# Gate and up projections by Strassen's algorithm, down projection accumulated in DRAM

## The chip, the cores and the metric

The kernel runs on one core of a Trainium2 chip. The metric is the device time of one execution in microseconds (us); of several runs the median is given. The core has five engines that run side by side, each through its own list of instructions in a fixed order: TensorE (PE; its weight loads are shown apart as PEld), VectorE (DVE), ScalarE (ACT), GpSimd (POOL) and SyncE (SP, which only issues DMAs here). An instruction that waits for another engine holds up all that stands behind it on its own.

## The reference

One layer of a decoder for 512 tokens of 2048 features, all in float32. The part that the change touches is the feed-forward network:

```python
z = rmsnorm(h, norm_ffn_g[l])
ff = (jax.nn.silu(z @ w_ffn_gate[l]) * (z @ w_ffn_up[l])) @ w_ffn_down[l]
h = h + ff.astype(h.dtype)
return rmsnorm(h, norm_final_g)
```

Gate and up are 2048 x 5632 each, down is 5632 x 2048. Ahead of it stand a combined input projection, windowed attention, gated linear attention, a gated merge and an output projection with the residual.

## The kernel before, in words

Everything lies with features on the 128 partitions and the 512 tokens along the row. The weights come in pieces of 128 x 1024 float32 (512 KB), in the order of their use; a piece holds, for gate, up and down alike, four blocks of 128 rows by 256 columns.

**Three matmuls for one.** TensorE multiplies in a format of fewer bits (F32R), so both sides are split into a high and a low part: ScalarE casts (high, L196), VectorE subtracts (low, L197). `mm3` (L229 to L233) then adds three products: high x high, high x low, low x high, each a matmul of 128 x 128 weights with 512 columns.

**Pieces.** `load_piece` (L203) asks for the DMA into `wf` and splits it into `wh` and `wl`, three buffers of each. `next_piece` (L217) hands out piece i and asks for the ones up to i + 2; it also takes up other waiting work of the attention part. `project` (L235) gives two banks of 256 output features.

**Feed-forward.** 5632 hidden features go in 11 blocks of 512. `ffn_up` (L856) makes gate and up of a block, in two halves of 256 features: four pieces of gate into two banks, then four of up; VectorE multiplies with the token's inverse rms (`rb2`), ScalarE gives the sigmoid, VectorE the products, and the result is split into `fh` and `fl`. `ffn_down` (L880) takes 8 pieces; for each of 16 output tiles 12 matmuls fill a bank, which VectorE adds to a running sum `acc` in SBUF (L892). The order is up(0), up(1), down(0), up(2), down(1) and so on; the last down is done in two halves of 256 tokens together with the final norm (L937 on).

**Buffers.** Eight banks of PSUM of 128 x 512 float32 take TensorE's results: four under the tag "mm" (all projections), four under "aux" (attention, norms). Tiles of 128 x 512 lie in 66 slots ("t") and 12 work tiles ("w"). A framework puts in all waits: a tile's buffer is given to the next one when its last reader is done, and a static scheduler fixes each engine's order.

In front of the feed-forward, the output projection (L821) leaves the residual stream in `hT`, sends it to DRAM (`h_d`, L827) and splits the gained z at once into `zh`, `zl` (L831 to L839), while the squares for the second norm are summed up.

## Time and profile before

| | us |
|---|---|
| median of three runs | 2664.93 |
| lowest, highest | 2664.81, 2666.26 |
| span of the profiled execution | 2663.9 |

The profile is one execution. Its span runs from the first to the last instruction of the core; the runs' times hold a little more around it, and 2664.93 less 2663.9 is 1.0 us. A page gives busy times by engine, the chain of work that ended last, and groups of instructions: line, engine, operation, what is written from what, count, then busy time and the mean length of one, and the engine's idle time just before them with what ended it. TensorE's matmuls overlap, so the length of one is not its price; that is the step from one start to the next. A timeline row has start and length in us. A row of the windows has, for a stretch, each engine's busy us and count, then PEclk, the TensorE clock that was granted (1.00 is full), the DMA share and GB/s.

### The profile page before, as it was taken

What the parts mean: (1) busy time and instruction counts of PE and PEld (TensorE: products, weight loads), DVE (VectorE), ACT (ScalarE), POOL (GpSimd) and SP (SyncE); (2) the same over time, 40 slices, a digit from 0 to 9 for tenths busy, and PEclk for the clock granted to TensorE, in tenths of its full rate; (3) what the DMA queues carried; (4) which work ended last, traced back from release to release, by engine and by line L of the source; (5) the groups of instructions that cost most, each with busy time, mean ns of one, the idle gap of its engine ahead of it and who ended that gap; (6) DMA issues with size and microseconds to landing.
All of it is one profiled execution on the core that took longest, in us unless ns stands there. A gap on an engine that the chain in (4) does not pass through costs nothing.

```text
span 2663.9 us, 29245 instructions
## 1 busy us (share of the span) xinstructions
PE 2635.0 (99%) x12038; PEld 2188.5 (82%) x12038; DVE 1185.7 (45%) x1690; ACT 753.0 (28%) x1040; POOL 21.4 (1%) x42
## 2 busy tenths in 40 slices
PE   8899999999999999999999999999999999999998
PEld 7777888888888888888888888888888888888887
DVE  6695463733333335444343434444434343434355
ACT  5465222422222223332222222222222222222233
POOL 0000000000000000000000000000000000000001
PEclk9999999999999999999999999999999999999999
DMA  6622223234433333443343233323323232233231
GB/s 193 130 71 71 80 87 95 72 127 133 127 111 111 108 98 107 142 147 103 99 141 117 95 98 101 95 95 96 102 95 95 96 101 96 95 96 102 95 124 67
DMA packets 92070, 280.73 MB, mean 105 GB/s; under 512 B 10512, under 2 KB 18880, under 8 KB 91936
## 3 DMA queue, kind: packets, MB, share of 16 engines
q1 hardware_dynamic: 91936, 278.87, 33.3%
q8 instruction: 94, 1.54, 0.2%
q14 instruction: 40, 0.33, 0.0%
HBM read 263.11 MB, written 15.72 MB: 105 GB/s over the span
## 4 chain that ended last, share of the span: by engine, by line
PE 96%; DMA 1%; DVE 1%; ACT 1%; issue 0%; POOL 0%; SPq 0%; DVEq 0%; ACTq 0%; POOLq 0%
PE ps_fd L232 6%; PE ps_fd L233 6%; PE ps_fd L231 6%; PE ps_fg L233 6%; PE ps_fg L231 6%; PE ps_fg L232 6%; PE ps_fu L233 6%; PE ps_fu L232 6%; PE ps_fu L231 6%; PE ps_ga L231 2%; PE ps_wo L233 2%; PE ps_gb L231 2%; PE ps_ga L232 2%; PE ps_wo L232 2%; PE ps_ga L233 2%; PE ps_gb L233 2%
## 5 line engine op out<-in xcount | busy, mean ns | idle before, releaser
L197 DVE TENSOR_TENSOR wl<-wf,wh 128x1024 fp32r<-128x1024 f32 (+1 forms) x464 | 559.0, 1205 | 1011.0 <-ACT wh L196 1002.6
L196 ACT CAST wh<-wf 128x1024 fp32r<-128x1024 f32 (+1 forms) x464 | 481.3, 1038 | 1535.6 <-PE ps_fd L232 315.5
L231 PE MATMUL ps_fu<-zh,wh 128*128 128x512 f32 x704 | 274.0, 389 | 0.0
L232 PE MATMUL ps_fu<-zl,wh 128*128 128x512 f32 x704 | 274.0, 389 | 0.0
L233 PE MATMUL ps_fu<-zh,wl 128*128 128x512 f32 x704 | 273.9, 389 | 0.0
L231 PE MATMUL ps_fg<-zh,wh 128*128 128x512 f32 x704 | 273.9, 389 | 0.0
L232 PE MATMUL ps_fg<-zl,wh 128*128 128x512 f32 x704 | 273.9, 389 | 0.0
L233 PE MATMUL ps_fg<-zh,wl 128*128 128x512 f32 x704 | 273.9, 389 | 0.0
L231 PE MATMUL ps_fd<-fh,wh 128*128 128x512 f32 x640 | 249.0, 389 | 0.0
L232 PE MATMUL ps_fd<-fl,wh 128*128 128x512 f32 x640 | 249.0, 389 | 0.0
L233 PE MATMUL ps_fd<-fh,wl 128*128 128x512 f32 x640 | 249.0, 389 | 0.0
L892 DVE TENSOR_TENSOR acc<-ps_fd,acc 128x512 f32<-128x512 f32 x160 | 110.5, 691 | 193.7 <-PE ps_fd L233 193.7
L232 PEld LDWEIGHTS ps_fg<-zl,wh 128*128 128x128 f32 x704 | 132.2, 188 | 27.4
L233 PEld LDWEIGHTS ps_fu<-zh,wl 128*128 128x128 f32 x704 | 132.2, 188 | 27.4
L233 PEld LDWEIGHTS ps_fg<-zh,wl 128*128 128x128 f32 x704 | 132.2, 188 | 27.4
L232 PEld LDWEIGHTS ps_fu<-zl,wh 128*128 128x128 f32 x704 | 132.2, 188 | 27.4
L231 PEld LDWEIGHTS ps_fg<-zh,wh 128*128 128x128 f32 x704 | 132.2, 188 | 27.4
L231 PEld LDWEIGHTS ps_fu<-zh,wh 128*128 128x128 f32 x704 | 132.2, 188 | 27.4
L231 PEld LDWEIGHTS ps_fd<-fh,wh 128*128 128x128 f32 x640 | 120.2, 188 | 25.0
L233 PEld LDWEIGHTS ps_fd<-fh,wl 128*128 128x128 f32 x640 | 120.2, 188 | 24.9
L232 PEld LDWEIGHTS ps_fd<-fl,wh 128*128 128x128 f32 x640 | 120.2, 188 | 24.9
L231 PE MATMUL ps_ga<-uh,wh 128*128 128x512 f32 x256 | 100.1, 391 | 0.0
(264 smaller groups left out, 3992.8 us busy)
## 6 DMA issues: line engine op xcount, KB each, us to landing
wf<-in_pieces_dram SPq DMA_DIRECT2D x448, 512.0 KB, 3.7
x<-in_xT_dram SPq DMA_DIRECT2D x16, 256.0 KB, 4.8
wf<-in_pieces_dram SPq DMA_DIRECT2D x16, 256.0 KB, 4.6
mA_d<-sga SPq DMA_DIRECT2D x16, 256.0 KB, 3.2
ya<-mA_d SPq DMA_DIRECT2D x16, 256.0 KB, 3.0
hT<-in_xT_dram SPq DMA_DIRECT2D x16, 256.0 KB, 3.6
h_d<-hT SPq DMA_DIRECT2D x16, 256.0 KB, 3.3
acc<-h_d SPq DMA_DIRECT2D x16, 256.0 KB, 4.8
```

The source lines that it names most:

```text
L196: nc.scalar.copy(dst_hi, src)
L197: nc.vector.tensor_tensor(out=dst_lo, in0=src, in1=dst_hi.bitcast(F32), op=ALU.subtract)
L231: nc.tensor.matmul(ps, lhsT=ah, rhs=bh, start=first, stop=False)
L232: nc.tensor.matmul(ps, lhsT=ah, rhs=bl, start=False, stop=False)
L233: nc.tensor.matmul(ps, lhsT=al, rhs=bh, start=False, stop=last)
L892: nc.vector.tensor_tensor(out=acc[m], in0=bank, in1=acc[m], op=ALU.add)
```

## The change

**Gate and up together by Strassen's algorithm (Winograd's form).** The left side is z: 512 tokens in two halves, times pairs of feature tiles (`za`, `zb`). The right side is a pair of weight blocks of gate and of up. Seven products replace eight; each has 256 tokens. A row of the tile `zs` holds the high part of such a left side in its first 256 columns and the low part in the others. One matmul of 512 columns multiplies both with the high weights, a second one of 256 columns adds low weights x high side onto the first half of the bank; the two halves of a bank are added when it is read ("fold").

**Weights.** A piece now holds, for four row blocks, 128 columns of gate and of up (quads). `load_quads` splits the first three quarters as they are, forms four sums in place, and splits all of it again: two tiles `wh` and two `wl` a piece, of four buffers each (three before); `wf` has two buffers (three before).

**One pair.** `ffn_pair` makes 128 hidden features from four pieces with seven banks: four aux (products 0, 2, 4, 6), three mm (1, 3, 5). VectorE then combines the banks, folds them and applies norm, sigmoid and product. A block has four pairs.

**Left sides.** `strassen_side` builds the seven sides for a pair of feature tiles; three of the eight pairs of tiles as the output projection goes on, five behind it. z is scaled by the first norm's `rb1`, and the second norm is divided by it again.

**Down.** Its bank is copied by ScalarE into a work tile, and GpSimd issues a DMA that adds it onto `h_d` in DRAM. The running sums are read back ahead of the last block. The order is four pairs of block 0, then for each block: the first pair of the next block, down, three more pairs. There are 11 work tiles instead of 12.

```diff
-N_LONG, N_SHORT = 66, 12
+N_LONG, N_SHORT = 66, 11
+KEPT = 6
...
+    def load_quads(i, wf, wh, wl):
+        nc.sync.dma_start(wf, pieces[i])
+        split(wh[:, 0 : 6 * P], wl[:, 0 : 6 * P], wf[:, 0 : 6 * P])
+        b11, b21, b22, b12 = (wf[:, n * 2 * P : (n + 1) * 2 * P] for n in range(4))
+        tt = nc.vector.tensor_tensor
+        tt(out=b11, in0=b11, in1=b12, op=ALU.add)
+        tt(out=b12, in0=b12, in1=b22, op=ALU.add)
+        tt(out=b22, in0=b11, in1=b22, op=ALU.add)
+        tt(out=b21, in0=b22, in1=b21, op=ALU.add)
+        th = wpool.tile([P, CW], F32R, tag="wh", name=f"th_{i}")
+        tl = wpool.tile([P, CW], F32R, tag="wl", name=f"tl_{i}")
+        split(th, tl, wf)
...
+    def strassen_side(j, za, zb):
+        s12, s34 = work(f"s12_{j}"), work(f"s34_{j}")
+        tt = nc.vector.tensor_tensor
+        tt(out=s12[:, one], in0=zb[:, two], in1=za[:, two], op=ALU.subtract)
...
+        for i, side_ in enumerate(sides):
+            t = slot(f"zs_{j}_{i}", F32R)
+            split(t[:, one], t[:, two], side_)
+            zs[j].append(t)
...
+        if m0 < KEPT:
+            strassen_side(m0 // 2, *pair)
+        else:
+            late.append((m0 // 2, *pair))
+    for pair in late:
+        strassen_side(*pair)
...
+    def ffn_pair(blk, j):
+        outs = [(mm_bank if i % 2 else aux_bank)(f"ps_fu{blk}_{j}_{i}") for i in range(7)]
+        for k0 in range(0, KD // 2, 2):
+            raw, sums = next_quads()
+            for i, (hl, at) in enumerate(
+                ((raw, 0), (raw, 1), (raw, 2), (sums, 0), (sums, 3), (sums, 2), (sums, 1))
+            ):
+                bank = outs[i]
+                for kp in range(2):
+                    k = k0 + kp
+                    z = zs[k][i]
+                    wh, wl = (t[:, at, kp] for t in hl)
+                    if k < KD // 2 - 1:
+                        nc.tensor.matmul(bank, lhsT=wh, rhs=z, start=k == 0, stop=False)
+                        nc.tensor.matmul(bank[:, one], lhsT=wl, rhs=z[:, one], start=False, stop=False)
+                    else:
+                        nc.tensor.matmul(bank[:, one], lhsT=wl, rhs=z[:, one], start=False, stop=False)
+                        nc.tensor.matmul(bank, lhsT=wh, rhs=z, start=False, stop=True)
...
+        nc.scalar.copy(u, outs[0])
+        tt(out=c, in0=outs[1], in1=u, op=ALU.add)
+        fold(g[:, one], c)
+        tt(out=u, in0=u, in1=outs[5], op=ALU.subtract)
+        tt(out=u3, in0=outs[4], in1=u, op=ALU.add)
+        tt(out=c2, in0=outs[6], in1=u3, op=ALU.add)
+        fold(g[:, two], c2)
+        tt(out=u3, in0=outs[3], in1=u3, op=ALU.add)
+        fold(up[:, two], u3)
+        tt(out=u, in0=outs[3], in1=u, op=ALU.add)
+        tt(out=u, in0=outs[2], in1=u, op=ALU.add)
+        fold(up[:, one], u)
+        tt(out=g, in0=g, in1=rb2, op=ALU.mult)
...
-                    mm3(bank, wh[:, j, ws], wl[:, j, ws], fh[j], fl[j], j == 0, j == 3)
-                if blk == 0:
-                    acc[m] = slot(f"acc_{m}")
-                    nc.sync.dma_start(acc[m], h_d[m])
-                nc.vector.tensor_tensor(out=acc[m], in0=bank, in1=acc[m], op=ALU.add)
+                    mm3(bank, wh[:, j, ws], wl[:, j, ws], *f[j], j == 0, j == 3)
+                part = work(f"fd_{blk}_{m}")
+                nc.scalar.copy(part, bank)
+                nc.gpsimd.dma_start(h_d[m], part, accum_op=ALU.add)
...
+    ff = [ffn_pair(0, j) for j in range(4)]
+    for blk in range(NB - 1):
+        nxt = [ffn_pair(blk + 1, 0)]
+        ffn_down(blk, ff)
+        nxt += [ffn_pair(blk + 1, j) for j in range(1, 4)]
+        ff = nxt
```

In the changed file, L208 and L209 are the split, L238 to L241 the four sums, L944 to L948 the product matmuls, L956 the fold of two halves, L958 ScalarE's copy of product 0, L959 to L976 the rest of the combination (L968 is the last reader of product 2, L972 allots the sigmoid's tile), L993 the copy of a down bank and L994 the accumulating DMA.

## The prediction

> **What bounds the kernel now.** I read the page first (busy shares, then the chain), then the groups by form, then TensorE's, VectorE's and the clock's rows in time.

> ```profile
> span 2663.9 us, 29245 instructions
> PE 2635.0 (99%) x12038; PEld 2188.5 (82%) x12038; DVE 1185.7 (45%) x1690; ACT 753.0 (28%) x1040; POOL 21.4 (1%) x42
> PE 96%; DMA 1%; DVE 1%; ACT 1%; issue 0%; POOL 0%; SPq 0%; DVEq 0%; ACTq 0%; POOLq 0%
> L231 PE MATMUL ps_fu<-zh,wh 128*128 128x512 f32 x704 | 274.0, 389 | 0.0
> ```

> TensorE is the bound, and its column "idle before" is 0.0: in gate and up (six groups of 704) it never waits. The 389 ns are the length of one overlapped matmul; the price is the step from start to start, so TensorE's timeline, the first and last of 31 matmuls of 512 columns and of 19 of 256 (with nothing else between):

> ```profile
> 1219.83 0.39 PE L233 MATMUL ps_fg<-zh,wl 128*128 128x512 f32 x1
> ...
> 1226.63 0.39 PE L233 MATMUL ps_fg<-zh,wl 128*128 128x512 f32 x1
> ...
> 2634.72 0.28 PE L231 MATMUL ps_fd<-fh,whd 128*128 128x256 f32 x1
> ...
> 2636.88 0.28 PE L231 MATMUL ps_fd<-fh,whd 128*128 128x256 f32 x1
> ```

> 6.80/30 = 0.2267 us and 2.16/18 = 0.120 us: the short one costs little over half, its own weight load included.

> **TensorE's work.** Before: 11 blocks x 8 feature tiles x 16 x 3 = 4224 steps, 957.6 us. Now: 44 pairs (one call of ffn_pair each) x 4 pieces x 7 products x 2, that is 2464 long and 2464 short steps, 2464 x 0.3467 = 854.3 us. Gain 103.3. A pair is 56 x 0.3467 = 19.4 us, a piece 4.85. [...]

> **VectorE's work.** Groups by form, then VectorE's timeline (first column start, second length):

> ```profile
> L197 DVE TENSOR_TENSOR wl<-wf,wh 128x1024 fp32r<-128x1024 f32 x448 | 548.2, 1224 | 1009.6 <-ACT wh L196 1001.2 <-PE ps_att L663 8.4
> L892 DVE TENSOR_TENSOR acc<-ps_fd,acc 128x512 f32<-128x512 f32 x160 | 110.5, 691 | 193.7 <-PE ps_fd L233 193.7
> L953 DVE TENSOR_TENSOR osum<-osum,osq 128x256 f32<-128x256 f32 x28 | 12.4, 442 | 10.7 <-ACT osq L951 10.7
> L196 ACT CAST wh<-wf 128x1024 fp32r<-128x1024 f32 x448 | 471.7, 1053 | 1531.6 <-PE ps_fd L232 315.5 <-PE ps_fg L232 299.3 <-PE ps_fu L232 203.2
> L735 ACT COPY ob<-ps_ob 128x512 f32<-128x512 f32 x8 | 4.7, 586 | 4.0 <-PE ps_ob L727 4.0
> ```
> ```profile
> 1512.81 0.69 DVE L873 TENSOR_TENSOR u<-ps_fu,rb 128x512 f32<-128x512 f32 x1
> 1513.54 0.69 DVE L874 TENSOR_TENSOR u<-u,g 128x512 f32<-128x512 f32 x1
> 1514.14 1.22 DVE L197 TENSOR_TENSOR wl<-wf,wh 128x1024 fp32r<-128x1024 f32 x1
> 1515.28 0.68 DVE L197 TENSOR_TENSOR fl<-u,fh 128x512 fp32r<-128x512 f32 x1
> ```

> Independent instructions overlap by 0.09: steps 0.60 (512) and 1.14 (1024); one that reads the result just ahead of it starts 0.73 behind. The same 0.09 off the lengths gives 0.36 for 256 columns and 0.87 for 768 (0.955 long, between the lengths for 512 and 1024). A piece now costs VectorE 0.87 + 4 x 0.36 + 1.14 = 3.45, where it cost 1.14; a pair's fold (L956 to L976 and one split) is 4 x 0.36 + 12 x 0.60 = 8.6. A pair asks 4 x 3.45 + 8.6 = 22.4 us of VectorE at the very least, against TensorE's 19.4. VectorE, 45% busy overall, becomes the slower engine in this stage; the projection down, where it has room, can prepare only two pieces ahead (four hi buffers, two a piece).

> **Where the wait lies.** Seven of eight banks are in use, and even-numbered products share four, so product 2 of a pair needs the bank whose last reader is L968 of the pair before. Before, on TensorE, gate to up, and now, pair 5_3 to pair 6_0 (block and pair):

> ```order
> L232 MATMUL ps_fg5_1_1_12760<-zl_15_8661,wh_323_12792 128x512
> L233 MATMUL ps_fg5_1_1_12760<-zh_15_8660,wl_323_12793 128x512
> L231 MATMUL ps_fu5_1_0_12891<-zh_0_7643,wh_324_12822 128x512 [waits Activation_49]
> L232 MATMUL ps_fu5_1_0_12891<-zl_0_7644,wh_324_12822 128x512
> L233 MATMUL ps_fu5_1_0_12891<-zh_0_7643,wl_324_12823 128x512 [waits DVE_49]
> ```
> ```order
> L948 MATMUL ps_fu5_3_6_15088<-zs_7_6_8864,th_335_15141 128x512
> L945 MATMUL ps_fu6_0_0_15285<-zs_0_0_7661,wl_336_15175 128x256 [waits DVE_49]
> L944 MATMUL ps_fu6_0_0_15285<-zs_1_0_7828,wh_336_15174 128x512
> L945 MATMUL ps_fu6_0_0_15285<-zs_1_0_7828,wl_336_15175 128x256
> L945 MATMUL ps_fu6_0_1_15286<-zs_0_1_7664,wl_336_15175 128x256
> L944 MATMUL ps_fu6_0_1_15286<-zs_1_1_7831,wh_336_15174 128x512
> L945 MATMUL ps_fu6_0_1_15286<-zs_1_1_7831,wl_336_15175 128x256
> L944 MATMUL ps_fu6_0_2_15287<-zs_0_2_7667,wh_336_15174 128x512 [waits DVE_49,PE_49]
> ```

> After a pair's end TensorE has 0.9 us of work, then stands at product 2 (the last row) with everything queued behind it. VectorE, the fold of pair 5_2 between loads of pieces (c, u, uu, u3, cc, g are the fold's tiles, wl and tl lows of raw and summed weights):

> ```order
> L959 TENSOR_TENSOR c_5_2_15058<-ps_fu5_2_1_14880,uu_5_2_15054 128x512 [waits DMASW5_49,PE_49,Activation_49]
> L956 TENSOR_TENSOR g_5_2_15056<-c_5_2_15058 128x256 [waits DMASW6_49,DMASW3_49,DVE_49]
> L209 TENSOR_TENSOR tl_331_14939<-wf_331_14928,th_331_14938 128x1024 [waits Activation_49]
> L209 TENSOR_TENSOR wl_332_14972<-wf_332_14970,wh_332_14971 128x768 [waits DMAHW7_49,Activation_49]
> L238 TENSOR_TENSOR wf_332_14970<-wf_332_14970 128x256 [waits DVE_49]
> L239 TENSOR_TENSOR wf_332_14970<-wf_332_14970 128x256 [waits DVE_49]
> L961 TENSOR_TENSOR uu_5_2_15054<-uu_5_2_15054,ps_fu5_2_5_14884 128x512 [waits DMASW4_49,PE_49]
> L240 TENSOR_TENSOR wf_332_14970<-wf_332_14970 128x256 [waits DVE_49]
> L962 TENSOR_TENSOR u3_5_2_15055<-ps_fu5_2_4_14883,uu_5_2_15054 128x512 [waits DMASW7_49,DVE_49]
> L241 TENSOR_TENSOR wf_332_14970<-wf_332_14970 128x256 [waits DVE_49]
> ```
> ```order
> L963 TENSOR_TENSOR cc_5_2_15059<-ps_fu5_2_6_14885,u3_5_2_15055 128x512 [waits DVE_49,PE_49]
> L956 TENSOR_TENSOR g_5_2_15056<-cc_5_2_15059 128x256 [waits DVE_49]
> L965 TENSOR_TENSOR u3_5_2_15055<-ps_fu5_2_3_14882,u3_5_2_15055 128x512
> L209 TENSOR_TENSOR tl_332_14981<-wf_332_14970,th_332_14980 128x1024 [waits Activation_49]
> L209 TENSOR_TENSOR wl_333_15014<-wf_333_15012,wh_333_15013 128x768 [waits DMAHW0_49,Activation_49]
> L956 TENSOR_TENSOR u_5_2_15057<-u3_5_2_15055 128x256 [waits DVE_49]
> L238 TENSOR_TENSOR wf_333_15012<-wf_333_15012 128x256 [waits DVE_49]
> L967 TENSOR_TENSOR uu_5_2_15054<-ps_fu5_2_3_14882,uu_5_2_15054 128x512
> L239 TENSOR_TENSOR wf_333_15012<-wf_333_15012 128x256 [waits DVE_49]
> L968 TENSOR_TENSOR uu_5_2_15054<-ps_fu5_2_2_14881,uu_5_2_15054 128x512 [waits DVE_49]
> ```

> From L959 to the end of L968: 7 x 0.60 + 9 x 0.36 + 2 x 1.14 + 2 x 0.87 = 11.5, with 0.4 for instructions that read their neighbour's result: 11.9 us. L959 in turn starts behind ScalarE's copy of product 0 (L958), and that product closes in the pair's fourth piece. So the pairs form a loop. From L968, TensorE has five products of the first piece (3.5), two pieces (9.7), two steps taken early (0.45) and the rest of product 0 (0.47): 14.1. The matmul's end adds 0.16 (0.39 less 0.227), the copy 0.6 (0.586 by L735). 11.9 + 14.9 = **26.8 us a pair instead of 19.4**, a gap of 7.4. Where the order puts product 3 ahead of product 2 (the second pair of a stage) it is 0.7 less, since one product fewer lies behind L968; I take 7.0 throughout. The first pair behind each projection down has two prepared pieces and does not wait; the down phases leave stages of 5, nine times 4, and 3 pairs, so 44 - 11 = 33 pairs wait: **+231 us**. Bounds: 11.9 could be 10.5 (neighbours' waits free, rows closer) or 13.5 (every instruction at 0.04 over its length), 33 x 1.5 = 50 either way.

> **The clock.** TensorE's timeline and the windows (PEclk is the column behind POOL) at its one long gap:

> ```profile
> 96.33 0.79 PE L231 MATMUL ps_qa<-uh,wh 128*128 128x512 f32 x1 [6.94 <-ACT wh L196]
> 96.92 0.63 PE L232 MATMUL ps_qa<-ul,wh 128*128 128x512 f32 x1
> 97.35 0.63 PE L231 MATMUL ps_qa<-uh,wh 128*128 128x512 f32 x1
> 97.77 0.63 PE L233 MATMUL ps_qa<-uh,wl 128*128 128x512 f32 x1
> ```
> ```profile
> 90.00:91.00 1.00, 0.00 (x0) 0.00 (x0) 0.00 (x0) 0.00 (x0) 0.00 (x0) 1.00 1.08 232
> 92.00:93.00 1.00, 0.00 (x0) 0.00 (x0) 0.00 (x0) 0.00 (x0) 0.00 (x0) 0.50 0.95 366
> 101.00:102.00 1.00, 1.00 (x4) 0.80 (x3) 0.97 (x2) 0.98 (x2) 0.00 (x0) 0.59 0.91 298
> 102.00:103.00 1.00, 1.00 (x9) 0.85 (x7) 0.97 (x6) 0.08 (x1) 0.00 (x0) 1.00 0.92 197
> ```

> The gap began at 89.39 (96.33 less 6.94); by 92 the granted clock is 0.50, and it stays there until about 101.6. For 5.3 us a step costs 0.425 (97.77 less 96.92, halved) instead of 0.227: 2.5 us lost. The loop's gaps are of that length (6 to 7.4), and what follows lies on the loop, so each should lose 0 to 2.5. I take 2.2, since some gaps are shorter: **+73 us**. [...]

> **Start and end.** Five of eight left sides are built behind the last output projection: 5 x 11 x 256 columns, some 20 us at 0.36, and the third piece's raw low stands behind them. TensorE covers two pieces (9.7) of it: about +14 (10 to 18). At the end no next pair hides the fold, and the last block's weights are split only behind it: from the pair's end some 9 us, a clock loss of 2, a point for the crowded first half: +12 (8 to 18).

> **What costs nothing.** ScalarE copies a down bank (0.586) inside the 2.7 us that TensorE takes for one (12 x 0.2267); VectorE loses L892. The 512 KB of a piece land in 3.7 us behind a free buffer, inside the five that VectorE takes for a piece; with two buffers instead of three there is about 1 us to spare, 33 to 44 us if it goes. Elsewhere one work tile less: 0 (-3 to +5).

> ```profile
> wf<-in_pieces_dram SPq DMA_DIRECT2D x448, 512.0 KB, 3.7
> h_d<-hT SPq DMA_DIRECT2D x16, 256.0 KB, 3.3
> ```

> An accumulating DMA isn't in the trace. The nearest row is a plain write of 256 KB, 3.3 us. ScalarE's later copies reuse a tile whose DMA was issued five banks (13.6 us) before, so the cost is 0 up to four times that row; beyond, the down phase slows. I take 0.

> **The sum.** The runs' median, 2664.9, is 1.0 over the span. 2663.9 + 1.0 - 103.3 + 231 + 73 + 14 + 12 = **2892 us**, called 2890.

> **Rivals.** *Faster:* L968 comes before product 2 is wanted, there is no loop, and 2664.9 - 103.3 + 26 = 2588. It decides at a chain of 11.9 us falling under about 4.5. For it, VectorE idles 55% now; against it, the 22.4 us that a pair asks. 5%. *Loop broken, VectorE saturated:* 22.4 a pair, 33 x 3.0 = 99, 2688; against it, the copy L958 that VectorE must await. 7%. *Loop at full clock:* gaps broken up by odd matmuls keep the clock at 1.00: 2819. For it, only that the trace has a single such gap. 18%. *Accumulation late:* at twice the plain row and one at a time, the twelfth lands 79 us behind the phase's start, and the first fold's last tile (L972) is that one's; it is wanted at some 64 (43.5 of down, 20 of a pair). Ten phases 15 us late: 3040. No row speaks for it. 8%. The forecast keeps 62%.

> **The numbers.** The forecast's own range is 2835 to 2960 (50 for the chain, 20 for the clock). Taking in the full-clock rival with its bound gives 2785 to 2960, leaving out 5 + 7 + 8%. Within 0.2% (5 us), about what a measurement here can tell from no change, only a saturated VectorE with a short start would land: 2%. Faster 6%, slower 92%.

> **What would show it.** Right: TensorE's waits headed by the product matmuls (L944) for VectorE's uu, some 33 of 6 to 9 us; PEclk of 8 or so in the gate and up slices; VectorE at some 1850 us busy (1185.7, less 176 loads of 1.224, 220 instructions of 0.69 and L892's 110.5, plus 176 x 3.95 + 44 x 10.1, lengths and not steps); L958 to L958 of neighbouring pairs 27 to 29 us. Wrong: pairs at 20 us with no gaps; gaps with PEclk at 1.00; ScalarE's L993 waiting for the POOL queue.

## The result and the profile after

The changed kernel takes **2768.8 us** (median of four runs, 2767.4 to 2772.0) against 2665.1 for the one before: 1.039 times as long, 95% interval 1.0376 to 1.0406. The forecast was 2890, with 2785 to 2960 as its range: slower, as said, but by 104 us and not by 225. The page of the profiled execution:

```profile
span 2766.2 us, 33264 instructions
PE 2603.9 (94%) x12742; PEld 2143.9 (78%) x12742; DVE 1774.0 (64%) x2984; ACT 994.0 (36%) x1460; POOL 160.4 (6%) x202
PEclk9999999999999999999999999999999999999998
PE 58%; DVE 23%; issue 12%; ACT 4%; DMA 2%; POOL 0%; ACTq 0%; DVEq 0%; SPq 0%; POOLq 0%
```

TensorE was 96% of the chain of work that ended last and is 58% now; VectorE has 23% of it. VectorE's 1774 us busy are near the forecast's 1850. The granted clock is where it was: no slice of gate and up shows the forecast's 8. TensorE's waits (total, times, longest, in us):

```profile
PE ps_fu L944 <- ACT th L208: 97.4, 113, 2.3
PE ps_fu L944 <- DVE u L962: 14.6, 32, 1.2
PE ps_fu L945 <- DVE wl L209: 11.1, 1, 11.1
```

There is no gap of 6 to 9 us behind VectorE's uu. There are over a hundred short ones, most of them before the first product of a piece's *sums* (th), for their cast. The second row is the wait at product 2: it ends with L962, not with L968, the reader of product 2 that the forecast named. A block in the windows: the pair behind a projection down, the second, the third, and the next block's first pair with the down behind it (second column length, then busy us of TensorE, its weight loads, VectorE, ScalarE, GpSimd; PEclk third from the end):

```profile
1798.43:1818.14 19.71, 19.71 (x113) 17.12 (x112) 13.84 (x21) 8.36 (x10) 0.86 (x1) 1.00 0.46 108
1818.14:1839.09 20.95, 18.61 (x102) 15.44 (x100) 18.81 (x35) 7.08 (x9) 0.00 (x0) 1.00 0.22 74
1839.09:1864.53 25.44, 21.70 (x113) 16.76 (x112) 23.17 (x41) 8.75 (x11) 0.00 (x0) 1.00 0.26 83
1864.53:1889.98 25.45, 21.74 (x113) 16.70 (x112) 23.12 (x41) 8.98 (x11) 0.00 (x0) 1.00 0.25 83
1889.98:1935.47 45.49, 45.49 (x206) 37.77 (x206) 24.37 (x34) 19.00 (x27) 13.00 (x15) 1.00 0.87 197
```

The four pairs and a down take 137.0 us; TensorE's own work in them is 4 x 19.4 + 43.5 = 121.1. So a block loses 15.9 us: nothing to speak of behind a down, 3.5 in the second pair (its window is short by some 2 us of matmuls, which the last row has), 6.0 in the third and 6.1 in the next block's first. Of such a 6.0 TensorE is idle for 3.7 (25.44 less 21.70); 2.0 lie in its busy time, 21.70 for matmuls that take 19.71 in the first row, at full clock, and 0.3 is the first row's own excess over 19.4. Where they wait, VectorE is busy for 23.2 of 25.4 us. In down itself TensorE never waits.

**What sets 25.4 us.** TensorE's waits in one such pair (timeline; the bracket has the idle time before the row and what ended it), two of VectorE's rows, and the chain of work through the same pair:

```profile
1563.79 1.19 PE L944 MATMUL ps_fu<-zs,th 128*128 128x512 f32 x4 [0.45 <-ACT th L208]
1568.65 0.47 PE L944 MATMUL ps_fu<-zs,wh 128*128 128x512 f32 x1 [0.41 <-DVE u L962]
1570.03 0.96 PE L944 MATMUL ps_fu<-zs,th 128*128 128x512 f32 x3 [0.44 <-ACT th L208]
1576.92 1.18 PE L944 MATMUL ps_fu<-zs,th 128*128 128x512 f32 x4 [1.18 <-ACT th L208]
1583.60 1.19 PE L944 MATMUL ps_fu<-zs,th 128*128 128x512 f32 x4 [1.17 <-ACT th L208]
```
```profile
1562.82 0.69 DVE L959 TENSOR_TENSOR c<-ps_fu,uu 128x512 f32<-128x512 f32 x1 [0.75 <-ACT uu L958]
...
1574.02 0.68 DVE L968 TENSOR_TENSOR uu<-ps_fu,uu 128x512 f32<-128x512 f32 x1
```
```profile
1581.96 0.44 DVE wf L241
...
1582.50 1.05 ACT th L208
...
1583.60 1.65 PE ps_fu L944 x6
...
1587.38 0.25 PE ps_fu L948
...
1587.65 0.60 ACT uu L958
...
1588.27 0.70 DVE c L959
```

The forecast's chain from L959 to the end of L968 was 11.9 us, and it is (1562.82 to 1574.70). But product 2 of the next pair starts at 1568.65, six us before L968 ends, on L962, the last reader of product 4. L968's bank goes to a later product, and all that waits for it are weight loads, 22 times in the run and 6.6 us together. The loop closes elsewhere. VectorE works without a long pause from L959 (1562.82) to the last weight sum of the next pair's third piece (L241, ends 1582.40): 19.6 us, the fold and the lows and sums of three pieces mixed in one queue. Then ScalarE casts these sums (1.05, with the hand-overs 1.2), TensorE does the rest of the third piece and the fourth's first product, which closes product 0 (4.0), ScalarE copies it (0.6), and the next L959 starts at 1588.27: 25.45 us. (The first expectation below calls this piece the fourth; it is the third.)

### The profile page after: what moved, and what is told of

Read it like the earlier page. It is cut to its first block, busy times and chain, and to the rows that moved or that the text cites. A ratio compares the mean times of both kernels' runs of the same rounds, so it can differ in the third digit from the quotient of the medians.

```text
span 2766.2 us, 33264 instructions
## 1 busy us (share of the span) xinstructions
PE 2603.9 (94%) x12742; PEld 2143.9 (78%) x12742; DVE 1774.0 (64%) x2984; ACT 994.0 (36%) x1460; POOL 160.4 (6%) x202
## 4 chain that ended last, share of the span: by engine, by line
PE 58%; DVE 23%; issue 12%; ACT 4%; DMA 2%; POOL 0%; ACTq 0%; DVEq 0%; SPq 0%; POOLq 0%
PE ps_fu L944 6%; PE ps_fd L270 6%; PE ps_fd L272 6%; PE ps_fd L271 6%; DVE wl L209 3%; DVE tl L209 3%; ACT th L208 3%; PE ps_fu L945 3%; PE ps_ga L270 2%; PE ps_ga L271 2%; PE ps_gb L270 2%; PE ps_ga L272 2%; PE ps_gb L272 2%; PE ps_gb L271 2%; PE ps_wo L271 2%
## 5 line engine op out<-in xcount | busy, mean ns | idle before, releaser
L209 DVE TENSOR_TENSOR wl<-wf,wh 128x1024 fp32r<-128x1024 f32 (+2 forms) x464 | 511.1, 1102 | 611.6 <-ACT wh L208 603.0
L208 ACT CAST wh<-wf 128x1024 fp32r<-128x1024 f32 (+2 forms) x464 | 442.3, 954 | 799.7 <-DMA wf<-in_pieces_dram 162.2
L944 PE MATMUL ps_fu<-zs,th 128*128 128x512 f32 x1232 | 433.7, 408 | 97.4 <-ACT th L208 97.4
L944 PEld LDWEIGHTS ps_fu<-zs,th 128*128 128x128 f32 x1232 | 222.6, 188 | 172.1 <-ACT th L208 133.6
L944 PE MATMUL ps_fu<-zs,wh 128*128 128x512 f32 x924 | 336.2, 402 | 16.9 <-DVE u L962 14.6
L208 ACT CAST th<-wf 128x1024 fp32r<-128x1024 f32 x176 | 184.5, 1048 | 461.1 <-DVE wf L241 297.4
L945 PE MATMUL ps_fu<-zs,tl 128*128 128x256 f32 x1232 | 313.4, 283 | 0.8 <-DVE tl L209 0.8
L209 DVE TENSOR_TENSOR tl<-wf,th 128x1024 fp32r<-128x1024 f32 x176 | 215.1, 1222 | 129.6 <-ACT th L208 117.7
L945 PE MATMUL ps_fu<-zs,wl 128*128 128x256 f32 x924 | 248.5, 282 | 11.1 <-DVE wl L209 11.1
L945 PEld LDWEIGHTS ps_fu<-zs,tl 128*128 128x128 f32 x1232 | 232.3, 189 | 28.5 <-DVE tl L209 13.7
L944 PEld LDWEIGHTS ps_fu<-zs,wh 128*128 128x128 f32 x924 | 171.9, 188 | 69.9 <-issue 23.2
L994 POOL DMA_DIRECT2D h_d<-fd x160 | 138.9, 912 | 1247.8 <-ACT fd L993 1242.0
L945 PEld LDWEIGHTS ps_fu<-zs,wl 128*128 128x128 f32 x924 | 175.0, 189 | 21.7 <-DVE wl L209 11.4
L993 ACT COPY fd<-ps_fd 128x512 f32<-128x512 f32 x160 | 90.8, 582 | 58.0 <-PE ps_fd L272 58.0
## 6 DMA issues: line engine op xcount, KB each, us to landing
wf<-in_pieces_dram SPq DMA_DIRECT2D x448, 512.0 KB, 3.3
h_d<-fd POOLq DMA_DIRECT2D x160, 256.0 KB, 6.0
x<-in_xT_dram SPq DMA_DIRECT2D x16, 256.0 KB, 4.7
wf<-in_pieces_dram SPq DMA_DIRECT2D x16, 256.0 KB, 4.3
mA_d<-sga SPq DMA_DIRECT2D x16, 256.0 KB, 2.8
ya<-mA_d SPq DMA_DIRECT2D x16, 256.0 KB, 2.9
hT<-in_xT_dram SPq DMA_DIRECT2D x16, 256.0 KB, 3.8
h_d<-hT SPq DMA_DIRECT2D x16, 256.0 KB, 3.4
```

The lines of the kernel that those rows point to most:

```text
L208: nc.scalar.copy(dst_hi, src)
L209: nc.vector.tensor_tensor(out=dst_lo, in0=src, in1=dst_hi.bitcast(F32), op=ALU.subtract)
L944: nc.tensor.matmul(bank, lhsT=wh, rhs=z, start=k == 0, stop=False)
L945: nc.tensor.matmul(bank[:, one], lhsT=wl, rhs=z[:, one], start=False, stop=False)
L993: nc.scalar.copy(part, bank)
L994: nc.gpsimd.dma_start(h_d[m], part, accum_op=ALU.add)
```

## Experiments

Two theories stood at first. **Q**: VectorE's whole in-order queue sets a waiting pair; whatever it sheds or gains per pair the pair does too, down to TensorE's 19.4. **B**: the forecast's loop, through the bank that L968 frees. The kernel before ran beside each experiment, at 2664.9 to 2665.3 us; runs without an interval are single ones.

**e1_two_more: more work for VectorE, behind L968.**

```diff
         fold(up[:, one], u)
+        for _ in range(2):
+            tt(out=c, in0=c2, in1=c2, op=ALU.add)
```

> Two more additions of 128x512 on VectorE in every pair, behind the fold that reads product 2 (nothing uses their result). Theory Q (VectorE's queue: the pair's time is VectorE's work from the first addition of the fold to the last weight sum of the next pair's fourth piece, 19.6 us, then the cast of those sums 1.05, TensorE's last piece 4.1 and ScalarE's copy 0.6, 25.4 together): 1.2 us more in each of the 34 pairs that have gaps now, +41 us, 2800 to 2815. Theory B (the prediction's loop through the bank that L968 frees): the additions stand behind L968, so 2769 as now, 2765 to 2775.

Measured 2838.4. B falls: work behind L968 costs. Q's 1.2 us is exact where the clock stays up (26.66 for 25.44), but the whole is 28 us above the 2810 that Q's 41 give. Windows of e1: such a pair and one that is longer with the same work, then two stretches of 3.41 us around the longest gap of the first and two around that of the second; and the rows that end these gaps in TensorE's timeline:

```profile
1442.01:1468.67 26.66, 21.74 (x114) 16.88 (x113) 24.38 (x43) 8.78 (x11) 0.00 (x0) 1.00 0.24 80
1871.43:1899.67 28.24, 23.31 (x114) 18.09 (x113) 24.38 (x43) 8.79 (x11) 0.00 (x0) 0.94 0.24 75
1458.11:1461.53 3.42, 1.67 (x9) 1.26 (x9) 2.73 (x6) 1.14 (x2) 0.00 (x0) 1.00 0.01 4
1461.53:1464.94 3.41, 2.83 (x15) 2.44 (x16) 2.78 (x4) 1.27 (x2) 0.00 (x0) 1.00 0.20 55
1888.18:1891.60 3.42, 1.14 (x9) 0.78 (x7) 2.16 (x6) 1.77 (x3) 0.00 (x0) 1.00 0.00 0
1891.60:1895.01 3.41, 3.41 (x9) 2.73 (x10) 3.28 (x5) 0.63 (x1) 0.00 (x0) 0.50 0.36 107
```
```profile
1462.11 1.19 PE L944 MATMUL ps_fu<-zs,th 128*128 128x512 f32 x4 [2.28 <-ACT th L208]
...
1891.54 2.04 PE L944 MATMUL ps_fu<-zs,th 128*128 128x512 f32 x4 [2.28 <-ACT th L208]
```

Both gaps are 2.28 us long. After the second the granted clock is 0.50 for 3.41 us, 1.6 us lost (28.24 less 26.66); after the first it stays at 1.00 (the last section shows where the two lie). Over the whole run e1's mean granted clock is 0.981 and the changed kernel's 0.993: of 2836.6 and 2766.2 us that is 53.9 and 19.4 us of clock not granted, some 34 more, enough for the 28. The forecast's clock loss exists, then, but the changed kernel's trace has the clock at 1.00 from 1229.6, in its first pair, to 2693.9, behind its last.

**e2_bank_early: product 2 read early.**

```diff
         tt(out=u, in0=u, in1=outs[5], op=ALU.subtract)
+        u2 = work(f"u2_{blk}_{j}")
+        tt(out=u2, in0=outs[2], in1=u, op=ALU.add)
...
-        tt(out=u, in0=outs[3], in1=u, op=ALU.add)
-        tt(out=u, in0=outs[2], in1=u, op=ALU.add)
-        fold(up[:, one], u)
+        tt(out=u2, in0=outs[3], in1=u2, op=ALU.add)
+        fold(up[:, one], u2)
```

> The fold reads product 2 right behind product 5, three positions and some 6 us earlier, into a tile of its own; as many VectorE instructions as now. Theory B (the bank of L968): the loop of 26.8 us falls below 21 and most gaps go, 2600 to 2680. Theory Q (VectorE's queue): nothing that the queue holds is less, 2755 to 2775, the lower end for TensorE's short waits at products 2 and 6 (0.4 us each).

Measured 2776.5: no gain, if anything 8 us lost, and the third pairs of a stage stay at 25.4. B falls a second time.

**e5_no_sums: the sums left out.**

```diff
-        tt(out=b11, in0=b11, in1=b12, op=ALU.add)
-        tt(out=b12, in0=b12, in1=b22, op=ALU.add)
-        tt(out=b22, in0=b11, in1=b22, op=ALU.add)
-        tt(out=b21, in0=b22, in1=b21, op=ALU.add)
```

> The four weight sums of each piece are left out (the last four products then use the plain weights); all else is as in the changed kernel. Theory Q (VectorE's queue): 16 x 0.36 to 0.44 us less in a pair, 25.4 falls to TensorE's 19.4 to 20, and of the 197 us of gaps in the 44 pairs some 160 go: 2590 to 2630. Theory G (the gaps come from something else on the way, the DMA of a piece or ScalarE's cast behind it): 2700 or more.

Measured 2598.7. A third pair of a stage in it:

```profile
1400.12:1419.83 19.71, 19.71 (x113) 17.14 (x112) 17.18 (x25) 8.99 (x11) 0.00 (x0) 1.00 0.32 106
```

With 6 us less for VectorE, TensorE is never idle in it (nor in any other pair but the first two): the landing of the pieces, the casts and the banks would all have kept up. This is what Q asks, but it isn't Q alone: the sums' place between a piece's two casts goes with their work, and e3 below parts the two. With the sums for nothing, this order of the work would be 66 us under the kernel before.

**e4_down_alone: the kernel before with the new down.** The running sums are read back ahead of the last block.

```diff
...
-                nc.vector.tensor_tensor(out=acc[m], in0=bank, in1=acc[m], op=ALU.add)
+                part = work(f"fd_{blk}_{m}")
+                nc.scalar.copy(part, bank)
+                nc.gpsimd.dma_start(h_d[m], part, accum_op=ALU.add)
```

> The kernel before with the new path of down alone: ScalarE copies each bank, GpSimd issues the adding DMA, the running sums are read back once ahead of the last block. Prediction's price of this part, 0: 2660 to 2670. If the adding DMAs or the copies were part of the loss: 2680 or more.

Measured 2672.4, 7 us more. Four of them are two waits early in the last down (first row, 1.2 and 2.5), for the cast of its weights, whose landings are issued between and behind the read-back's 16 transfers; this down's matmuls are busy for 2.4 us more as well (111.3 for 108.9 before). In the changed kernel the adding DMAs land in 6.0 us (second row), nearly twice the plain write's 3.4, and no listed wait is for them.

```profile
L231 PE MATMUL ps_fd<-fh,whd 128*128 128x256 f32 x128 | 37.4, 292 | 4.0 <-ACT whd L196 3.8 <-DVE acc L948 0.2
```
```profile
h_d<-fd POOLq DMA_DIRECT2D x160, 256.0 KB, 6.0
```

**e12_three_landing: three buffers for the landing piece, nine work tiles.**

```diff
-N_LONG, N_SHORT = 66, 11
+N_LONG, N_SHORT = 66, 9
...
-        wf = wpool.tile([P, CW], F32, tag="wf", name=f"wf_{i}", bufs=2)
+        wf = wpool.tile([P, CW], F32, tag="wf", name=f"wf_{i}", bufs=3)
```

> The changed kernel with three landing buffers as before the change instead of two (nine work tiles instead of eleven). Theory Q: VectorE's queue has the same work, so nothing: 2755 to 2775. If the two buffers cost the 33 to 44 us that the prediction put on them in case: 2725 to 2740.

Measured 2762.9. Of the 6 us, 4.6 are gained ahead of the feed-forward (its first matmul starts at 1199.4 instead of 1204.1); the pairs are as long as before. Two landing buffers cost the changed kernel nothing in the pairs, as forecast.

**e3_sums_pool: the sums on GpSimd**, in `load_quads`.

```diff
-        tt = nc.vector.tensor_tensor
+        tt = nc.gpsimd.tensor_tensor
```

> The four sums of a piece (L238 to L241) go on GpSimd instead of VectorE. Theory Q: VectorE loses 16 x 0.36 to 0.44 = 5.8 to 7.0 us a pair, 25.4 falls to TensorE's 19.4 plus small gaps, and some 150 of the 197 us of gaps go: 2600 to 2640, under the kernel before, if GpSimd takes no more than the 0.75 us of its one 128x256 row each (3.2 us a piece against 4.85 on TensorE). Theory B: only the nine sums between L959 and L968 count, 3.2 us a pair, 2650 to 2680. If GpSimd's sums slow down VectorE, or stand behind its DMA issues in the down stages, above 2680.

Measured 2937.0 (1.102, interval 1.1003 to 1.104), 300 us off. Q as stated counted work and forgot the order. The chain through one piece of e3:

```profile
1959.50 1.05 ACT th L208
...
1960.57 0.59 DVE tl L209
...
1961.71 0.68 DVE fl L209
1962.40 0.88 DVE wl L209
...
1963.35 0.74 POOL wf L238
...
1965.78 0.74 POOL wf L241
...
1966.55 1.06 ACT th L208
```

From one cast of sums to the next 7.05 us pass: VectorE's queue holds the next piece's low behind this piece's, the sums wait for that low, the cast for the sums. While VectorE stands for GpSimd it can't go on to another piece. (Part of the 168 us over the changed kernel is the clock: the mean granted clock is 0.969 here and 0.993 there.) Q needs the clause that a piece's steps form a chain through this queue.

**e7_ahead: the split of the sums issued behind the next piece's raw split.**

```diff
...
-        split(th, tl, wf)
+        if pending:
+            split(*pending.pop())
+        pending.append((th, tl, wf))
...
```

> The split of a piece's sums is issued behind the raw split of the next piece, so that VectorE has the next piece's low (0.87 us) to do while ScalarE casts the sums (1.05 us). Theory Q with the waits in VectorE's own order (1.19 us once a pair behind the last sum, 0.75 for ScalarE's copy): 25.4 falls to about 24.2, 34 x 1.2 = 40 us less, 2720 to 2740. If only the work in the queue counts, not its order: 2760 to 2775.

Measured 2915.6, far off again. ScalarE's waits for a landed piece, of e7 and of the changed kernel:

```profile
ACT wh L208 <- DMA wf<-in_pieces_dram: 750.3, 218, 18.5
```
```profile
ACT wh L208 <- DMA wf<-in_pieces_dram: 162.2, 70, 18.3
```

The landing buffer is free only when the low of its sums is done; that low now stands behind the next piece's, so with two buffers a landing starts too late.

**e8_ahead_pool: the edits of e7, e3 and e12 together.**

> As in e7_ahead, and the sums on GpSimd (0.81 us each from start to start in e3_sums_pool), with three buffers for the pieces as they land and nine work tiles. A piece's chain no longer runs through the split of the piece before: VectorE has 4 x 2.0 + 8.6 = 16.6 us a pair, GpSimd 13, TensorE 19.4, so TensorE should set the pair: 2600 to 2650. If GpSimd's sums still stand between two pieces of VectorE's queue (as in e3, 7.2 us a piece): 2800 or more.

Measured 2683.7, better than the change by 85 and short of the forecast by 34. The two chains are cut (most waiting pairs take 21.4 to 23.3 us), but VectorE's lows and GpSimd's sums take longer where they run side by side. Two of VectorE's lows, the first almost without and the second with sums on GpSimd beside it, and GpSimd's rows around the second (VectorE is idle from 1694.53 to 1696.25):

```profile
1681.08 0.96 DVE L209 TENSOR_TENSOR wl<-wf,wh 128x768 fp32r<-128x768 f32 x1
...
1697.66 1.49 DVE L209 TENSOR_TENSOR wl<-wf,wh 128x768 fp32r<-128x768 f32 x1
1699.07 0.68 DVE L965 TENSOR_TENSOR c<-ps_fu,uu 128x512 f32<-128x512 f32 x1
```
```profile
1695.10 0.73 POOL L240 TENSOR_TENSOR wf<-wf 128x256 f32<-128x256 f32 x1
1695.91 0.74 POOL L241 TENSOR_TENSOR wf<-wf 128x256 f32<-128x256 f32 x1
1696.73 1.60 POOL L242 TENSOR_TENSOR wf<-wf 128x256 f32<-128x256 f32 x1
1698.41 1.33 POOL L243 TENSOR_TENSOR wf<-wf 128x256 f32<-128x256 f32 x1
```

The low goes from 0.96 to 1.49, the sums from 0.73 to 1.60; L965, which reads a PSUM bank, keeps its 0.68 beside a sum. Over the whole run a low of 768 columns takes 1.16 us in e8 and 0.95 in e3.

**e6_quarters: down spread between the pairs.** The order of a block becomes pair, quarter of down (four output tiles), four times; three pairs' results stay in work tiles until the last quarter is done. The pieces are laid out in the same order.

```diff
+PLAN = [([0], 2), ([1], 2), ([2], 2), ([3], 2)]
...
+        for js, nd in PLAN:
+            for j in js:
+                up = ffn_pair(blk + 1, j)
...
+            ffn_down(blk, ff, c0, nd)
...
```

> The same instructions in another order: each of the four pairs of a block is followed by a quarter of the projection down (four output tiles, 10.9 us of TensorE) instead of all of down behind the first pair; the split of three pairs' results waits until down's last quarter is done. Theory Q: a pair and a quarter ask 25.8 us of VectorE (23.5 and two lows of 1.14) against 30.6 of TensorE, so the gaps of blocks 1 to 10 (some 160 us) fall to 20 to 60 and block 0 keeps its 35: 2620 to 2670, at or under the kernel before. Theory G: the gaps stay with the pairs, 2740 to 2770.

Measured 2700.3 (1.0129, interval 1.0112 to 1.0146): 68 us less with the same instructions, 30 short of the range. The chain of e6 in a stretch that waits:

```profile
1846.74 1.24 DVE tl L211
...
1847.99 4.76 DMA wf<-in_pieces_dram
...
1852.85 0.84 ACT wh L210
...
1853.71 0.97 DVE wl L211
...
1856.63 1.06 ACT th L210
...
1857.71 1.24 DVE tl L211
```

From split to split 11 us on two buffers, 5.5 a piece: the landing, which costs the changed kernel nothing, is the next limit once VectorE has room.

**e11_quarters_three: e6 with three landing buffers** as in e12. The tiles c, cc and gs share one, so that nine work tiles do.

```diff
...
-        u, u3, g, up, c, c2 = (work(f"{n}_{blk}_{j}") for n in ("uu", "u3", "g", "u", "c", "cc"))
+        u, u3, g, up, c = (work(f"{n}_{blk}_{j}") for n in ("uu", "u3", "g", "u", "c"))
+        c2 = c
...
```

> e6_quarters with three landing buffers instead of two (nine work tiles, the tiles c, cc and gs of the combination share one). In e6 the chain ran from the split of a piece's sums through the next landing (3.2 to 4.8 us), cast, low, sums, cast and split again, 10.9 us for two buffers, 5.4 a piece. With three it is 3.6 a piece, so theory Q leaves VectorE's 25.8 against 30.6: of the 129 us of gaps in e6 35 stay with block 0 and 15 to 50 with the others: 2620 to 2665. If the landing is not what held e6: 2690 to 2705.

Measured **2630.5** (0.987, interval 0.9855 to 0.9885): faster than both kernels, with the change's own matmuls. A pair with its quarter:

```profile
1471.96:1502.57 30.61, 30.61 (x161) 26.14 (x161) 25.02 (x41) 12.02 (x16) 3.44 (x4) 1.00 0.59 138
```

**e9_three_short: the high and low left sides in matmuls of their own, no fold.**

```diff
-                        nc.tensor.matmul(bank, lhsT=wh, rhs=z, start=k == 0, stop=False)
-                        nc.tensor.matmul(bank[:, one], lhsT=wl, rhs=z[:, one], start=False, stop=False)
...
+                    mm3(bank[:, one], wh, wl, z[:, one], z[:, two], k == 0, k == KD // 2 - 1)
...
```

> One part undone: instead of one matmul of 512 columns for the high and low left sides and halves added afterwards, three matmuls of 256 columns a product, all into the bank's first half; no fold, and the combination reads 256 columns. TensorE: 0.360 us a product step instead of 0.347, 20.2 us a pair, +33 over 44 pairs. VectorE: 7 x 0.60 + 4 x 0.36 become 7 x 0.36 to 0.44, 2.5 to 3.1 us a pair less. Theory Q: 25.4 falls to 22.3 to 23, some 34 x 2.7 = 90 us less against 8 us more in the ten pairs that do not wait: 2675 to 2705. If TensorE's work counts (theory T: gaps stay as they are): 2800.

Measured 2700.0 (1.0129, interval 1.0113 to 1.0144), 69 us less. Giving TensorE 0.4 us a pair more (20.15 without gaps, for 19.71) and VectorE some three less is a gain: the 512-column matmul saves on TensorE, where there is room, and spends on VectorE, where there is none.

**e10_short_quarters: the edits of e9, e6 and e12 together.**

> e9_three_short with down in quarters behind the pairs (e6_quarters), three landing buffers and nine work tiles. A pair and a quarter: VectorE 21.3 + 2.3 = 23.6 us against TensorE's 31.1, the landing no longer on two buffers. Theory Q: the gaps of blocks 1 to 10 go, 44 x 20.2 = 889 for gate and up (957.6 before, 69 less), plus 25 at start and end, 10 to 20 for block 0, 10 to 20 of rests: 2640 to 2660, at or just under the kernel before. If the landing of the pieces still sets the pace as in e6: 2680 or more.

Measured **2626.1** (0.9856, interval 0.9839 to 0.9872), 14 under the range; the fastest. Its pair and quarter take 31.06 us with TensorE busy throughout, as e11's 30.61; its first block, which has no down beside it, waits less.

## Why the prediction was wrong

| term | forecast, us | measured, us |
|---|---|---|
| gate and up on TensorE | -103 | -93 |
| gaps of the 33 waiting pairs | +231 | about +169 |
| clock in these gaps | +73 | 0 |
| start (the first pair's gaps) | +14 | +15 |
| end | +12 | +11 |
| sum | +227 | +102 (span 2766.2 less 2663.9) |

The measured column is from TensorE's start times in the timeline: a stretch's length less what its matmuls take without gaps. In a pair without gaps a product step takes 19.71/56 = 0.352 us and not 0.3467, 13 us in 44 pairs; the kernel before was 3 us over its 957.6.

**Right.** VectorE becomes the slower engine of the stage; a waiting pair takes far longer than TensorE's 19.4 (26.8 forecast, 25.4 measured); the pair behind a down doesn't wait; accumulation and ScalarE's copies cost little (7 us by e4, 0 forecast), the two landing buffers nothing; start and end.

**The step that failed** is this one: "product 2 of a pair needs the bank whose last reader is L968 of the pair before". Banks aren't handed on by position: product 2 waits for L962, 0.4 us. From this step came one gap of 7 us a pair at one place, and from the length of that gap the clock's 73 us. What there is instead is a chain through the preparation of the weights, which stops TensorE some five times a pair for 0.4 to 1.2 us, at PEclk 1.00. The rows on VectorE's need ("at the very least" 22.4) held most of the answer: in the changed kernel VectorE is busy for 23.2 us of such a pair and waits for ScalarE for 0.75 and 1.19, which makes 25.1 of the 25.4. The rival "VectorE saturated" was priced at its lower bound, where nothing waits on anything. That 26.8 came out near 25.4 is chance: the loop behind it is not there.

**The clock** was the larger miss, 73 of the 125 us between the two sums, and its rival ("loop at full clock", 2819) was nearest to the outcome. Second pairs that lose 3.5 and not 7, and the others' 6.0, make up 62 (the table counts 0.3 of each with the longer product steps); those steps took 10 back.

**The range.** Its lower ends stand above their own bounds: 2892 less 50 and 20 is 2822 and not 2835, and the full-clock rival's 2819 less 50 is 2769 and not 2785. A range down to 2769 would have ended at the measured time, but by chance: its loop would have been no better. The 20 us for the clock are the author's estimate, which no run shows; in these gaps the changed kernel lost nothing to the clock (PEclk 1.00 from 1238 to 2690).

## What to carry to other kernels

For a change that hands work from the bound engine to another, add up that engine's whole queue for one unit of the loop, with its waits for the third engine, and compare it with what stands *beside that unit* in time, not with its average share: here the same instructions were 104 us slower than before behind one long down, and 35 us faster in quarters between the pairs with three landing buffers. And each cut uncovers the next chain (bank, queue, landing, GpSimd beside VectorE): a price for one resource holds only while the one ahead of it stands.

## What the runs showed of the hardware

**The granted clock.** In the changed kernel a long gap stands at the start (11.1 us for wl, ended at 1226.1); from 1219.35, within it, to 1229.59 the clock is at 0.50, and then it is back at 1.00 (windows):

```profile
1227.00:1228.00 1.00, 1.00 (x6) 0.90 (x5) 1.00 (x4) 0.00 (x0) 0.00 (x0) 0.50 0.00 0
...
1230.00:1231.00 1.00, 0.39 (x2) 0.35 (x3) 0.41 (x1) 1.00 (x2) 0.00 (x0) 1.00 0.00 0
```

```profile
1215.94:1219.35 3.41, 0.00 (x0) 0.00 (x0) 3.41 (x11) 1.87 (x7) 0.00 (x0) 1.00 0.00 0
2690.50:2693.91 3.41, 1.33 (x9) 0.92 (x7) 2.34 (x4) 0.00 (x0) 0.00 (x0) 1.00 0.91 284
2751.94:2755.35 3.41, 1.41 (x10) 1.27 (x11) 1.07 (x4) 0.42 (x1) 0.70 (x1) 1.00 0.00 0
2516.42:2519.83 3.41, 1.85 (x9) 1.57 (x10) 2.22 (x4) 1.78 (x2) 0.00 (x0) 1.00 0.00 0
```

Ahead of the three falls TensorE is idle for 3.41, 2.08 and 2.00 us of a stretch; no stretch of the pairs between 1238 and 2690 has more than 1.56, and there the clock is 1.00 throughout. The 2.33 us are parted by the grid into 1.39 and 0.94. The four windows in e1 above are stretches of that length too: 3.42 less 1.14 is 2.3 idle, and the next one is at 0.50; 3.42 less 1.67 is 1.75, and the next one, into which the rest of that gap falls, is at 1.00.

These are times in the traces; what sets the clock they don't show, and no experiment moved a gap across the grid on purpose.

**GpSimd beside VectorE.** In e8 a sum takes 0.73 us while VectorE is idle and 1.60 beside two of its lows, and a low of 768 columns 1.49 beside sums for 0.96 almost without: there, moving elementwise work to an idle GpSimd was worth less than its idle share had promised (2683.7, for a forecast of 2600 to 2650).
